# First product of an MLP by seven block products instead of eight, in an encoder block on one core

## The chip, the cores and the metric

The kernel runs on one core of a Trainium2 chip. The metric is the device time of one execution in microseconds (us). Two kernels are compared by the median of several runs of each on the same chip.

The core's engines each work through a queue of their own in order: TensorE (PE, matmul; PEld is its weight load), VectorE (DVE), ScalarE (ACT), GpSimd (POOL), and SyncE (SP), which here only issues transfers. They meet at semaphores. PSUM, where matmuls leave their sums, has eight banks of 128x512 float32.

## The reference

One encoder block on 1536 tokens (512 + 1024) of width 1024, all in float32. Projections, gates and two kinds of attention come first; what the change touches is the end:

```python
merged = sigmoid(ga) * (oa @ w_branch_a) + sigmoid(gb) * (ob @ w_branch_b)
x = x + merged @ w_out
hm = rmsnorm(x, norm_mlp)
u = relu(hm @ w_up)            # 1024 -> 4096
return x + (u * u) @ w_down    # 4096 -> 1024
```

## The kernel before

A float32 product is made of three float16 matmuls: each operand is scaled and split into a high and a low half (`split16`, L924: ACT writes `hi`, DVE writes `lo = scale*src - hi`), and `mm3` (L173) adds hi·hi (L174), hi·lo (L175) and lo·hi (L176) in one PSUM bank. A matmul has 128 rows of weights, up to 512 columns of the moving operand, and a weight load before it.

The program is written as generator functions in one order, and a scheduler with a cost model of its own then sets the order of instructions on each engine's queue. On the chip each queue runs in that order and waits where it must.

The stages after attention, with the trace's times:

- **Branch products** (`branch`, L986; from 1000.30). Six raw weight tiles `st_b0` to `st_b5` are loaded into the pool `raw` (six slots of 128x1024 float32) and split into `w_b` in the pool `w16` (eight slots of [2,1024] float16). `load_o` transposes the attention output and splits it into `u16` and `u16b`.
- **Output projection** (`outproj`, L1009; from 1110.50). It has two halves of 512 output columns, each over three blocks `b` of 512 tokens; `op` matmuls use 512 columns and `y[t] += ...` is one DVE instruction (`add_scaled`, L943). In half 1, from 1173.16, `hnorm(tt)` (L1022) makes the normed rows `hm` of a tile of 128 tokens: two ACT squares with accumulator, small DVE steps, a power on POOL (`hr`), two DVE products. `htrans(tt)` (L1036) turns them: eight 128x128 transposes into two PSUM banks (`hT`), then per bank one ACT copy to `xp` high and one DVE subtraction to `xp` low. The last four tiles' transposes stand inside the first `up`.
- **MLP** (from 1244.33 to the end): a loop over c = 0 to 15, 256 hidden columns each, written as `up(c,0)`, `down_parts(c)`, `up(c,1)`, `up_parts(c+1)`, `up_norms(c+2)`, `down(c)`.
  - `up(c,i)` (L1109): for each block of 512 tokens 8 k-slices times 3 matmuls (72 in all), then for each block ACT `Relu` from PSUM (L1121), ACT square (L1122), ACT copy to `u` high (L1124), DVE subtraction to `u` low (L1125). The temporary `r` comes from the pool `t2` (seven slots of 128x512).
  - `down(c)` (L1127): 12 token tiles times 2 halves; 6 matmuls of 512 columns each into one bank, then `add_scaled` on DVE.
  - `up_norms(c+2)` (L1067): loads two row blocks of w_up as `st_n` (each 512 KB), ACT squares with accumulator (`sq`), one small matmul `nu`, DVE and POOL steps, which give the weights' scale `su` and the row factor `alpha`. `up_parts` (L1086): loads `st_u`, splits into `w_u`, two splits of 128x1024. `down_parts` (L1091): loads `st_d`, squares them, a small matmul `fro_d`, scale `rowd`, splits into `w_d`, two of 128x1024. All these raw tiles share the six `raw` slots, and SP issues their loads in order, each when its slot is free.

Of the kernel before, what the change touches and what calls it, by code (L numbers as in the profile page):

```python
# [130 lines left out]
def encoder(ctx, tc, xt, x, wg, wp, wb, wo, wu, wn, wd, nv, nvr, nmlp, nq, rpb, t5, oneh, negrow, cmask, yp, ys):  # L131
# [781 lines left out]
    with ExitStack() as es:  # L913
# [4 lines left out]
        def tmp(name):  # L918
            return pp.tile([P, 512], F32, tag="t2", bufs=7, name=name)
# [8 lines left out]
        def raw(name, src):  # L928
            st = pp.tile([P, D], F32, tag="raw", bufs=6, name=f"st_{name}")
            xch["last"] = nc.sync.dma_start(out=st, in_=src).ins  # L930
            return st

        def parts(name, st, scale, lo_eng):
            w = pp.tile([P, 2, D], F16, tag="w16", bufs=8, name=f"w_{name}")
            split16(w[:, 0], w[:, 1], st, scale, lo_eng)
            return w

        def squares(acc, st, scale=1.0):
            sq = pp.tile([P, D], F32, tag="sq", bufs=1, name="sq")
# [26 lines left out]
        def load_o(b):  # L966
# [319 lines left out]
```

## Time and profile before

| what | value |
|---|---|
| median of 3 runs | 2255.27 us (2252.01 to 2257.3) |
| the profiled execution: its own time | 2253.47 us |
| its span in the trace | 2251.6 us |
| PE busy | 2132.5 us, 95% |
| DVE, ACT, POOL busy | 1241.7 (55%), 1007.3 (45%), 365.9 us (16%) |
| first `br` matmul, first `op`, `op` half 1, first `up`, last `dn` | 1000.30, 1110.50, 1173.16, 1244.33, 2247.44 us |

How to read it: "busy" is the time in which an engine executes; a matmul's end is modelled, so that two matmuls in a row overlap in the records (each lasts 0.38 us, the next one starts 0.22 us after it). The pace of matmuls is therefore read from their starts. The granted clock is the share of TensorE's full speed (2.4 GHz) that the chip allowed; its lower level is 1.2 GHz. A name such as `up<-xp,w_u` gives output and inputs without buffer numbers. `[3.71 <-ACT sqm L1000]` behind a row says that the engine sat idle 3.71 us before it, and what released it.

### The profile page before, as it was taken

To read this page: it belongs to the slowest core of one execution; us is meant where nothing else is said; L and a number is where in the kernel's file an instruction comes from. 1 tells how busy PE (TensorE), PEld (TensorE's weight loads), DVE (VectorE), ACT (ScalarE), POOL (GpSimd) and SP (SyncE) were. 2 spreads that over 40 slices of the span, in tenths; PEclk is the share of its full clock that TensorE was granted. 3 is DMA by queue.
4 is the path that set the end of the run, shared out by engine and by line. 5 is a ranking of instruction groups with operands and counts; after the bars stand their busy time and mean duration, and the time that the engine had idled before them with its cause. 6 is when DMAs were issued, how large, how long until landed. Compare 5 with 4: busy or idle time off the path is not lost.

```text
span 2251.6 us, 32277 instructions
## 1 busy us (share of the span) xinstructions
PE 2132.5 (95%) x11440; PEld 1087.5 (48%) x11440; DVE 1241.7 (55%) x3135; ACT 1007.3 (45%) x2435; POOL 365.9 (16%) x541
## 2 busy tenths in 40 slices
PE   5899999899989999899999999999999999999999
PEld 3355555465555555344444544444444444444444
DVE  7546767676576577556644644444444444444444
ACT  6346765476566566346532533232333333323222
POOL 5123334244234244100000000000000000000000
PEclk9899999999999999999999999999999999999999
DMA  6676666887776776887530111101111111110002
GB/s 206 208 235 141 138 135 142 172 167 164 160 166 130 164 151 142 184 255 219 164 111 21 56 57 54 36 24 56 57 57 56 56 57 57 56 38 24 34 1 113
DMA packets 342187, 251.23 MB, mean 112 GB/s; under 512 B 210432, under 2 KB 302464, under 8 KB 342024
## 3 DMA queue, kind: packets, MB, share of 16 engines
q1 hardware_dynamic: 341878, 249.15, 42.8%
q8 instruction: 90, 1.47, 0.3%
q14 instruction: 73, 0.60, 0.1%
q10 hardware_dynamic: 146, 0.01, 0.0%
HBM read 164.02 MB, written 53.29 MB: 97 GB/s over the span
## 4 chain that ended last, share of the span: by engine, by line
PE 54%; DMA 1%; issue 1%; ACT 1%; DVE 1%; SPq 0%; POOL 0%; ACTq 0%; DVEq 0%; POOLq 0%
PE up L174 7%; PE dn L174 7%; PE dn L176 7%; PE up L176 7%; PE up L175 7%; PE dn L175 7%; PE op L174 2%; PE op L175 2%; PE op L176 2%; PE br L174 1%; PE br L176 1%; PE br L175 1%; DMA z<-z_d 1%; DMA st_b<-in_wb 0%; PE hT L1041 0%
## 5 line engine op out<-in xcount | busy, mean ns | idle before, releaser
L943 DVE SCALAR_TENSOR_TENSOR y<-dn,und,y 128x512 f32<-128x512 f32 x384 | 287.1, 750 | 179.3 <-PE dn L176 178.9
L1121 ACT ACTIVATE r<-up,alpha 128x512 f32<-128x512 f32 x96 | 65.2, 680 | 591.3 <-PE up L176 591.3
L174 PE MATMUL up<-xp,w_u 128*128 128x512 f16 x768 | 291.0, 379 | 1.0 <-ACT xp L1044 1.0
L176 PE MATMUL dn<-w_d,u 128*128 128x512 f16 x768 | 291.1, 379 | 0.0
L176 PE MATMUL up<-xp,w_u 128*128 128x512 f16 x768 | 291.0, 379 | 0.0
L175 PE MATMUL dn<-w_d,u 128*128 128x512 f16 x768 | 291.0, 379 | 0.0
L175 PE MATMUL up<-xp,w_u 128*128 128x512 f16 x768 | 291.0, 379 | 0.0
L174 PE MATMUL dn<-w_d,u 128*128 128x512 f16 x768 | 291.0, 379 | 0.0
L1125 DVE TENSOR_TENSOR u<-r,u 128x512 f16<-128x512 f32 x96 | 66.4, 692 | 285.1 <-ACT u L1124 281.6
L174 PE MATMUL g<-act,w_g 128*128 128x512 f16 x384 | 147.2, 388 | 21.9 <-ACT act L802 13.0
L175 PE MATMUL g<-act,w_g 128*128 128x512 f16 x384 | 148.3, 386 | 7.6 <-DVE act L803 7.6
L176 PE MATMUL g<-act,w_g 128*128 128x512 f16 x384 | 148.3, 386 | 1.1 <-DVE w_g L263 0.9
L174 PE MATMUL pj1b<-w_p,act 128*128 128x384 f16 x384 | 127.4, 332 | 7.6 <-DVE qn0b L380 4.3
L175 PEld LDWEIGHTS <-act 128*128 128x128 f16 x960 | 96.6, 101 | 70.8 <-issue 19.5
L176 PEld LDWEIGHTS <-act 128*128 128x128 f16 x960 | 96.1, 100 | 66.5 <-issue 7.1
L174 PEld LDWEIGHTS <-act 128*128 128x128 f16 x960 | 97.3, 101 | 63.8 <-issue 6.7
L175 PE MATMUL pj1b<-w_p,act 128*128 128x384 f16 x384 | 127.1, 331 | 0.0
L176 PE MATMUL pj1b<-w_p,act 128*128 128x384 f16 x384 | 127.1, 331 | 0.0
L189 POOL TENSOR_TENSOR f_d<-f_d,mhalf 128x1 f32<-128x1 f32 x16 | 8.9, 556 | 682.8 <-DVE f_d L196 682.8
L174 PEld LDWEIGHTS <-u 128*128 128x128 f16 x768 | 76.3, 99 | 88.9
L174 PEld LDWEIGHTS <-w_u 128*128 128x128 f16 x768 | 76.5, 100 | 88.5
L176 PEld LDWEIGHTS <-u 128*128 128x128 f16 x768 | 75.1, 98 | 90.7
(331 smaller groups left out, 4351.9 us busy)
## 6 DMA issues: line engine op xcount, KB each, us to landing
st_n<-in_wn SPq DMA_DIRECT2D x32, 512.0 KB
st_u<-in_wu SPq DMA_DIRECT2D x32, 512.0 KB
st_d<-in_wd SPq DMA_DIRECT2D x32, 512.0 KB
st_p<-in_wp SPq DMA_DIRECT2D x80, 192.0 KB
z_d<-z SPq DMA_DIRECT2D x48, 256.0 KB
z<-z_d SPq DMA_DIRECT2D x48, 256.0 KB
ba1a<-ba_d SPq DMA_DIRECT2D x12, 768.0 KB
xt<-in_xt SPq DMA_DIRECT2D x24, 256.0 KB
```

The lines of the kernel that those rows point to most:

```text
L174: nc.tensor.matmul(ps, ah, bh, start=first, stop=False)
L175: nc.tensor.matmul(ps, ah, bl, start=False, stop=False)
L176: nc.tensor.matmul(ps, al, bh, start=False, stop=last)
L189: nc.gpsimd.tensor_tensor(out=out, in0=in_, in1=mhalf[:, 0:in_.shape[1]], op=ALU.pow)
L943: nc.vector.scalar_tensor_tensor(out=out, in0=ps, scalar=scale, in1=out, op0=ALU.mult, op1=ALU.add)
L1121: nc.scalar.activation(s, ps[b], AF.Relu, scale=alpha[:, f:f + 1])
L1125: nc.vector.tensor_tensor(out=uu[:, 1, i, tb], in0=s, in1=uu[:, 0, i, tb], op=ALU.subtract)
```

## The change

The first product of the MLP, `up`, is made by Strassen's scheme (Winograd's form): tokens are cut in two halves of 768, the 1024 inputs in two halves of 512, the 256 hidden columns of a c in its two tiles of 128. Seven products of sums of blocks take the place of eight products of blocks. The sums are made in float32 and then split.

- `up(c,j)` now goes over j, two column blocks of 384 tokens of each half. It has seven products of 4 k-slices times 3 matmuls of 384 columns: 84 matmuls, 168 per c (before 144 of 512 columns). Their PSUM results are combined by one ACT copy (L1197) and seven DVE additions of 384 columns (L1193), and `hidden` (L1169 to L1174) does what L1121 to L1125 did, four times per j on 384 columns: three ACT and one DVE instruction each.
- `up_parts(c)` adds four POOL additions or subtractions of 128x512 (`s1` to `s4`) and makes seven splits of 128x512 (an ACT and a DVE instruction each; before two of 128x1024).
- `build(q)` takes the place of `htrans`: six builds of 256 tokens, each with 16 transposes into four banks, one ACT copy (`b12`), four DVE subtractions (`t1` to `t4`), and seven ACT copies to high and seven DVE subtractions to low, all of 128x512. Builds 0 to 3 stand behind the pairs of tiles of output projection half 1, builds 4 and 5 inside `up(0,0)` behind products 6 and 5; `hnorm(10)` and `hnorm(11)` come behind build 4.
- Buffers: `raw` has 4 slots (before 6), `t2` has 6 (7); `w16` 13 of [2,512] (8 of [2,1024]); `sq` is bfloat16. 14 slots `six` hold `u16b`, the output projection's weights and `xp`, and later the seven operands `xs` of each j. Branch weights `b4` and `b5` are loaded when `b0` and `b1` have been split.
- `outproj` takes one PSUM bank per token tile when its turn comes. `down` and its 144 matmuls per c stay, with the token tiles in another order; its weights are split in halves (four splits of 128x512).

```diff
-            return pp.tile([P, 512], F32, tag="t2", bufs=7, name=name)
+            return pp.tile([P, 512], F32, tag="t2", bufs=6, name=name)
...
-            st = pp.tile([P, D], F32, tag="raw", bufs=6, name=f"st_{name}")
+            st = pp.tile([P, D], F32, tag="raw", bufs=4, name=f"st_{name}")
...
+        def build(q):
+
+            tp = {}
+            for h in range(2):
+                for i in range(2):
+                    ps = tp[i, h] = psum(f"hT{2 * q + h}_{i}")
...
+            def out(name, src):
+                p4 = src.rearrange("p (k t) -> p k t", k=4)
+                hi, lo = (xs[name, j][:, l, :, cs] for l in range(2))
                 nc.scalar.activation(hi, p4, AF.Copy)
                 nc.vector.tensor_tensor(out=lo, in0=p4, in1=hi, op=ALU.subtract)
...
+            out("b11", tp[0, 0])
+            b12 = tmp(f"b12_{q}")
+            nc.scalar.activation(b12, tp[0, 1], AF.Copy)
+            t1 = less("t1", b12, tp[0, 0])
+            t2 = less("t2", tp[1, 1], t1)
+            out("t2", t2)
+            out("b21", tp[1, 0])
+            out("t1", t1)
+            t3 = less("t3", tp[1, 1], b12)
+            out("t3", t3)
+            out("b22", tp[1, 1])
+            out("t4", less("t4", tp[1, 0], t2))
...
+            s1 = sum_(tmp(f"s1_{c}"), a21, a22, ALU.add)
+            s2 = sum_(tmp(f"s2_{c}"), s1, a11, ALU.subtract)
+            out(1, a11)
+            out(6, s2)
+            out(2, a12)
+            out(5, s1)
+            s3 = sum_(a21, a11, a21, ALU.subtract)
+            s4 = sum_(a12, a12, s2, ALU.subtract)
+            yield
+            out(7, s3)
+            out(3, s4)
+            out(4, a22)
...
+                ps = psum(f"up{c}_{j}{n}")[:, :384]
+                for k in range(4):
                     kk = slice(k * P, (k + 1) * P)
+                    mm3(ps, w[:, 0, kk], w[:, 1, kk], x7[:, 0, k, :], x7[:, 1, k, :], k == 0, k == 3)
...
+            c11 = t384("c11_")
+            nc.scalar.activation(c11, product7(1), AF.Copy)
+            yield
+            x = add(t384("x_"), product7(6), c11)
+            yield
+            add(c11, product7(2), c11)
+            hidden(c, 0, 0, j, c11)
+            yield
+            p5 = product7(5)
+            yield
+            v = add(t384("v_"), product7(7), x)
+            c22 = add(t384("c22_"), p5, v)
+            add(x, p5, x)
+            hidden(c, 1, 1, j, c22)
+            yield
+            add(x, product7(3), x)
+            hidden(c, 0, 1, j, x)
+            yield
+            add(v, product7(4), v)
+            hidden(c, 1, 0, j, v)
```

Three places in the queues show the order. Names: `hm8_0` is the first half of tile 8's normed rows, `x_t41` the operand t4 of j = 1, `up0_06` product 6 of `up(0,0)`, `hs`, `hr` the norm's small sums and factors; before, `xp0` to `xp2` are the operands of the three token blocks.

PE in the first `up`, before: block 0, then the transposes of tiles 8 and 9 behind the first matmul of block 1.

```order
L176 MATMUL up0_0_14791<-xp0_12805,w_u0_14350 128x512
L174 LDWEIGHTS w_u0_14350 [waits DVE_49]
L174 MATMUL up0_1_14792<-xp1_12806,w_u0_14350 128x512 [waits Activation_49]
L1041 MATMUL hT8_0_14852<-ident_94,hm8_0_14692 128x128 [waits DVE_49,PE_49]
L1041 MATMUL hT8_0_14852<-ident_94,hm8_0_14692 128x128 x3
L1041 MATMUL hT8_1_14859<-ident_94,hm8_1_14693 128x128 [waits DVE_49,PE_49]
L1041 MATMUL hT8_1_14859<-ident_94,hm8_1_14693 128x128 x3
```

PE at the same place after: products 1 and 6 of `up(0,0)`, then the 16 transposes of build 4.

```order
L176 MATMUL up0_06_14928<-x_t20_14353,w_u0_6_14388 128x384
L1057 MATMUL hT8_0_14942<-ident_94,hm8_0_14882 128x128 [waits DVE_49]
L1057 MATMUL hT8_0_14942<-ident_94,hm8_0_14882 128x128 x3
L1057 MATMUL hT8_1_14947<-ident_94,hm8_1_14883 128x128 [waits DVE_49]
L1057 MATMUL hT8_1_14947<-ident_94,hm8_1_14883 128x128 x3
L1057 MATMUL hT9_0_14952<-ident_94,hm9_0_14893 128x128 [waits DVE_49,Activation_49]
```

What stood behind 24 products of block 0 now stands behind the 24 shorter matmuls of products 1 and 6, and waits for `hm8` as before.

DVE ahead of those transposes, before: `hm8` has one low half of `htrans` between the small steps ahead of it and itself.

```order
L1027 TENSOR_TENSOR hs9_14702<-hs9_14702 128x1 [waits Activation_49]
L1028 TENSOR_SCALAR hs9_14702<-hs9_14702 128x1 [waits DVE_49]
L1045 TENSOR_TENSOR xp1_12806<-hT6_0_14763,xp1_12806 128x4x128 [waits PE_49,Activation_49]
L1032 SCALAR_TENSOR_TENSOR hm8_0_14692<-y8_12801,hr8_14698,gm_12653 128x512 [waits Pool_49]
L1032 SCALAR_TENSOR_TENSOR hm8_1_14693<-y8_12801,hr8_14698,gm_12653 128x512
```

DVE at the same place after:

```order
L1069 TENSOR_TENSOR t4_3_14877<-hT6_1_14842,t2_3_14863 128x512
L1065 TENSOR_TENSOR x_t11_14834<-t1_3_14861,x_t11_14834 128x4x128 [waits Activation_49]
L1065 TENSOR_TENSOR x_t31_14836<-t3_3_14871,x_t31_14836 128x4x128 [waits Activation_49]
L1065 TENSOR_TENSOR x_b221_14832<-hT7_1_14852,x_b221_14832 128x4x128 [waits Activation_49]
L1041 TENSOR_TENSOR hs8_14881<-hs8_14881 128x1 [waits Activation_49]
L1065 TENSOR_TENSOR x_t41_14833<-t4_3_14877,x_t41_14833 128x4x128 [waits Activation_49]
L1042 TENSOR_SCALAR hs8_14881<-hs8_14881 128x1 [waits DVE_49]
L1041 TENSOR_TENSOR hs9_14892<-hs9_14892 128x1 [waits Activation_49]
L1042 TENSOR_SCALAR hs9_14892<-hs9_14892 128x1 [waits DVE_49]
L1046 SCALAR_TENSOR_TENSOR hm8_0_14882<-y8_12819,hr8_14888,gm_12653 128x512 [waits Pool_49]
```

The whole of build 3 (eleven DVE instructions, of which the last are shown) now stands ahead of `hm8`.

ACT in the second half of an up, before (c = 5: `up11_0` to `up11_2` are its blocks, `st_n8` the row blocks for c = 8, `st_d14` a down weight of c = 7):

```order
L925 ACTIVATE w_u13_17183<-st_u13_17181,su_12658 128x1024 [waits DMAHW0_49]
L1121 ACTIVATE r11_0_17113<-up11_0_17086,alpha_12657 128x512 [waits PE_49]
L1122 ACTIVATE r11_0_17113<-r11_0_17113 128x512 [waits Activation_49]
L1124 ACTIVATE u16_12652<-r11_0_17113 128x512 [waits Activation_49]
L940 ACTIVATE sq_17613,nu_12655<-st_n8_0_17611 128x1024 [waits DMAHW7_49]
L1121 ACTIVATE r11_1_17142<-up11_1_17087,alpha_12657 128x512 [waits PE_49]
L940 ACTIVATE sq_17617,nu_12655<-st_n8_1_17615 128x1024 [waits DMAHW0_49,Activation_49]
```

ACT at the same place after (c = 5, j = 1; `c11`, `c22` are two of the four results, `st_n7` the row blocks for c = 7, `st_d12` and `st_d13` the down weights of c = 6):

```order
L1197 ACTIVATE c11_5_1_17721<-up5_11_17722 128x384 [waits PE_49]
L925 ACTIVATE w_u6_1_17848<-st_u12_17840,su_12658 128x512 [waits DMAHW7_49]
L944 ACTIVATE sq_17873,nu_12655<-st_n7_0_17871 128x1024 [waits DMAHW1_49]
L1171 ACTIVATE c11_5_1_17721<-c11_5_1_17721,alpha_12657 128x384 [waits DVE_49]
L944 ACTIVATE sq_17877,nu_12655<-st_n7_1_17875 128x1024 [waits DMAHW2_49,Activation_49]
L1172 ACTIVATE c11_5_1_17721<-c11_5_1_17721 128x384 [waits Activation_49]
L1174 ACTIVATE u16_12652<-c11_5_1_17721 128x384 [waits Activation_49]
L944 ACTIVATE sq_18203,nd_12656<-st_d12_18201,nu_12655 128x1024 [waits DMAHW3_49]
L1171 ACTIVATE c22_5_1_17797<-c22_5_1_17797,alpha_12657 128x384 [waits DVE_49]
L944 ACTIVATE sq_18207,nd_12656<-st_d13_18205,nu_12655 128x1024 [waits DMAHW4_49,Activation_49]
```

The squares of `st_n` and `st_d`, with their waits for transfers, now stand between the steps of `hidden`; the norms of a c are taken one c nearer to their use.

## Rows read from the trace of the kernel before

**Rows 1.** First part of the page: busy time, share of the span and instructions of each engine.

```profile
PE 2132.5 (95%) x11440; PEld 1087.5 (48%) x11440; DVE 1241.7 (55%) x3135; ACT 1007.3 (45%) x2435; POOL 365.9 (16%) x541
```

**Rows 2.** Waits of PE from 1000 us to the end: what it waited for, us in total, times, the longest.

```profile
PE fro_m L194 <- ACT sqm L1000: 5.4, 2, 3.7
PE br L175 <- DVE u L926: 1.6, 1, 1.6
PE br L174 <- ACT u L925: 1.2, 1, 1.2
PE up L174 <- ACT xp L1044: 1.0, 1, 1.0
PE hT L1041 <- DVE hm L1032: 1.0, 2, 0.5
```

**Rows 3.** Timeline of PE in a steady `up`: start, modelled duration. The second row here is the 54th start behind the first, with no gap between.

```profile
1514.41 0.38 PE L174 MATMUL up<-xp,w_u 128*128 128x512 f16 x1
...
1526.06 0.38 PE L174 MATMUL up<-xp,w_u 128*128 128x512 f16 x1
```

**Rows 4.** Timeline of PE in the attention stage, matmuls of 384 columns: the second row is the 23rd start behind the first.

```profile
407.43 0.33 PE L174 MATMUL pj0b<-w_p,act 128*128 128x384 f16 x1
...
411.16 0.33 PE L176 MATMUL pj0b<-w_p,act 128*128 128x384 f16 x1
```

**Rows 5.** Costliest groups by line and shape: busy us, mean ns of one, idle before.

```profile
L174 PE MATMUL up<-xp,w_u 128*128 128x512 f16 x768 | 291.0, 379 | 1.0 <-ACT xp L1044 1.0
L174 PE MATMUL pj1b<-w_p,act 128*128 128x384 f16 x384 | 127.4, 332 | 7.6 <-DVE qn0b L380 4.3
```

**Rows 6.** Windows: stretch, length, busy time of PE, PEld, DVE, ACT and POOL with instructions, granted clock, DMA share, GB/s. The first lies in the attention stage, the second in the MLP, the third behind a gap of PE.

```profile
400.00:412.00 12.00, 11.49 (x85) 7.24 (x83) 6.53 (x38) 2.33 (x10) 1.21 (x3) 1.00 0.84 183
1600.00:1660.00 60.00, 60.00 (x283) 27.51 (x281) 26.43 (x44) 19.28 (x30) 1.95 (x3) 1.00 0.17 53
1045.50:1049.00 3.50, 3.50 (x13) 1.50 (x14) 1.67 (x5) 3.09 (x7) 0.55 (x1) 0.70 0.02 6
```

**Rows 7.** Groups by line and shape on DVE, ACT and POOL: busy us, mean ns of one, idle before.

```profile
L943 DVE SCALAR_TENSOR_TENSOR y<-dn,und,y 128x512 f32<-128x512 f32 x384 | 287.1, 750 | 179.3 <-PE dn L176 178.9
L1125 DVE TENSOR_TENSOR u<-r,u 128x512 f16<-128x512 f32 x96 | 66.4, 692 | 285.1 <-ACT u L1124 281.6
L926 DVE SCALAR_TENSOR_TENSOR w_u<-st_u,su,w_u 128x1024 f16<-128x1024 f32 x32 | 39.6, 1280 | 0.0
L1045 DVE TENSOR_TENSOR xp<-hT,xp 128x512 f16<-128x512 f32 x24 | 16.0, 686 | 1.2 <-ACT xp L1044 0.8
L1032 DVE SCALAR_TENSOR_TENSOR hm<-y,hr,gm 128x512 f32<-128x512 f32 x24 | 16.9, 746 | 2.6 <-POOL hr L189 2.6
L380 DVE TENSOR_TENSOR qn1b<-pj1b,rq1b 128x256 f32<-128x256 f32 x48 | 20.1, 419 | 4.1 <-POOL rq1b L375 3.6
L801 DVE TENSOR_TENSOR xt<-xt,rmsr 128x512 f32<-128x512 f32 x18 | 19.9, 1167 | 0.1
L1121 ACT ACTIVATE r<-up,alpha 128x512 f32<-128x512 f32 x96 | 65.2, 680 | 591.3 <-PE up L176 591.3
L244 ACT ACTIVATE wsq<-st_p 128x384 bf16<-128x384 f32 x80 | 41.4, 517 | 39.7 <-DMA st_p<-in_wp 39.1
L925 ACT ACTIVATE w_u<-st_u,su 128x1024 f16<-128x1024 f32 x32 | 34.8, 1133 | 0.0
L814 POOL TENSOR_TENSOR acc<-acc,sqx 128x512 f32<-128x512 f32 x14 | 19.2, 1373 | 5.6 <-ACT sqx L812 5.1
```

**Rows 8.** Timeline of SP in the MLP: when the loads of a round were issued, and the first of the next round.

```profile
1643.73 1.52 SPq L930 DMA_DIRECT2D st_u<-in_wu  x2
1646.12 1.52 SPq L930 DMA_DIRECT2D st_n<-in_wn  x2
...
1706.16 1.52 SPq L930 DMA_DIRECT2D st_u<-in_wu  x2
```

**Rows 9.** Timelines in the MLP: PE's `fro_d` matmul, and the splits of `w_d` that follow it on ACT and DVE (two rounds ahead of rows 8, same place of a round).

```profile
1514.27 0.28 PE L194 MATMUL fro_d<-nd,ones 128*128 128x2 f32 x2
...
1516.38 2.17 ACT L925 ACTIVATE w_d<-st_d,rowd 128x1024 f16<-128x1024 f32 x2
...
1517.55 2.48 DVE L926 SCALAR_TENSOR_TENSOR w_d<-st_d,rowd,w_d 128x1024 f16<-128x1024 f32 x2 [0.35 <-ACT w_d L925]
```

**Rows 10.** Timeline of ACT behind the loads of rows 8: the squares of the first `st_n` and of the second `st_d`.

```profile
1651.33 1.06 ACT L940 ACTIVATE sq<-st_n 128x1024 f32<-128x1024 f32 x1 [3.93 <-DMA st_n<-in_wn]
...
1658.79 1.15 ACT L940 ACTIVATE sq<-st_d,nu 128x1024 f32<-128x1024 f32 x1 [0.85 <-DMA st_d<-in_wd]
```

**Rows 11.** Timelines in output projection half 1: PE's transposes of three tiles, then of the fourth; and one DVE `add_scaled`, with DVE's idle time before it.

```profile
1214.60 2.78 PE L1041 MATMUL hT<-ident,hm 128*128 128x128 f32 x24
1217.88 1.32 PE L1041 MATMUL hT<-ident,hm 128*128 128x128 f32 x8 [0.49 <-DVE hm L1032]
...
1204.44 0.75 DVE L943 SCALAR_TENSOR_TENSOR y<-op,uo,y 128x512 f32<-128x512 f32 x1 [4.43 <-PE op L176]
```

**Rows 12.** Timeline of PE in the branch stage: a gap, and matmuls of 512 columns behind it.

```profile
1045.42 0.39 PE L194 MATMUL fro_m<-msum,ones 128*128 128x8 f32 x2 [3.71 <-ACT sqm L1000]
...
1047.00 0.63 PE L174 MATMUL br<-u16b,w_b 128*128 128x512 f16 x1
...
1049.99 0.54 PE L175 MATMUL br<-u16b,w_b 128*128 128x512 f16 x1
```

More of the change, by code (lines that the diff above doesn't have):

```diff
@@ L1058, in gains @@
         def gains():
[L1060 removed]
+            g2 = pp.tile([P, D], F32, tag="raw", bufs=4, name="g2")
             nc.vector.tensor_tensor(out=g2, in0=gm, in1=gm, op=ALU.mult)
@@ L1082, in up_norms @@
[L1082 to L1089 removed]
+            nc.vector.tensor_reduce(out=t[:, 0:1], in_=ps[:, :2], axis=AX.X, op=ALU.add)
@@ L1146, in encoder @@
         next(lo_)
-        wbs = [raw(f"b{k}", wb[k]) for k in range(6)]
+        wbs = [raw(f"b{k}", wb[k]) for k in range(4)]
         for _ in fill:
@@ L1152, in encoder @@
         sb = scale_b[:, 1:2]
-        wbs = [parts(f"b{k}", w, sb, nc.vector) for k, w in enumerate(wbs)]
+        for k in range(6):
+            wbs[k] = parts(f"b{k}", wbs[k], sb, nc.vector)
+            if k < 2:
+                wbs.append(raw(f"b{k + 4}", wb[k + 4]))
         eg.close()
@@ L1190, in encoder, with slots @@
                 todo, sc = scaled(wo1)
-                so[1] = [parts(*w, nc.vector) for w in todo], sc
+                so[1] = [w for t in todo for w in parts(*t, nc.vector)], sc
         up_norms(0)
-        for b in range(NB):
-            outproj(b, 1)
-            for t in range(4 * b, 4 * b + 4):
-                hnorm(t)
-            if b:
-                for t in range(4 * b - 4, 4 * b):
-                    htrans(t)
-            if b == 0:
-                up_parts(0)
-            if b == 1:
+        first = up_parts(0)
+        def slots(j):
+            for n in X_OF.values():
+                xs[n, j] = six(f"x_{n}{j}", [P, 2, 4, 384])
+        outproj(0, 1)
+        slots(0)
+        for t in range(2):
+            hnorm(t)
+        next(first)
+        for q in range(4):
+            outproj(1 + q // 2, 1, range(q % 2 * 2, q % 2 * 2 + 2))
+            if q == 3:
+                slots(1)
+            build(q)
+            for t in (2 * q + 2, 2 * q + 3):
+                hnorm(t)
+            if q == 1:
                 up_norms(1)
+        for _ in first:
+            pass
         NC = FF // 256
         for c in range(NC):
-            for i in range(2):
-                up(c, i, range(8, 12) if c == i == 0 else ())
-                if i == 0:
+            for j in range(2):
+                for i, _ in enumerate(up(c, j)):
+                    if c == j == 0 and i in (1, 3):
+                        build(4 + i // 2)
+                        if i == 1:
+                            hnorm(10)
+                            hnorm(11)
+                if j == 0:
                     down_parts(c)
             if c + 1 < NC:
-                up_parts(c + 1)
+                for _ in up_parts(c + 1):
+                    pass
             if c + 2 < NC:
```

139 lines of the change are left out of this document (80 added, 59 removed).

## The prediction

> **What bounds the kernel now.** I first read the busy shares: PE 2132.5 us of a span of 2251.6, 95%, DVE 55%, ACT 45%, POOL 16% [rows 1]. A share is an average over stages, so next the waits of PE from the branch products on: 10.2 us of about 1250 in all [rows 2], none of them in the MLP loop behind its first round. There PE sets the end, by the pace at which matmuls start. The timeline gives that pace: 54 starts in 11.65 us, 0.2157 us for 512 columns [rows 3]. A round of the loop (one c) takes 62.43 us [rows 8], and 288 matmuls at 0.2157 are 62.1; a few small ones are the rest. So time leaves this kernel only where PE gets less to do, or loses waits.
>
> **Part 1, the products.** Per c, 144 matmuls of 512 columns go and 168 of 384 come. The reader must not price them by the mean durations: 379 and 332 ns [rows 5] would give 54.6 us before and 55.8 after, a loss of 1.2 us per c. Matmuls overlap in the records, and the pace counts. For 384 columns the attention stage shows it: 23 starts in 3.73 us, 0.1622 [rows 4], at granted clock 1.00 [rows 6], with the same float16 operands and a weight load each. Before: 144 x 0.2157 = 31.06 us; after: 168 x 0.1622 = 27.25; saved 3.81 per c, 16 x 3.81 = 60.9 us. The new matmuls would break even at 31.06/168 = 0.185 us. The `down` half keeps its 144 matmuls (31.06 us); its other token order costs nothing that a row shows. The new round is 62.43 - 3.81 = 58.6 us.
>
> **Part 2, what the other engines must do in a round of 58.6 us.** DVE: 24 `add_scaled` x 0.75, 14 additions of 384 columns at about 0.55 (between 0.42 for 256 columns and 0.69 for 512), 8 low halves of 384 at 0.55, 11 splits of 512 at 0.75 less overlap, small steps: 18 + 8 + 4 + 8 + 2 = 40 us [rows 7]. ACT: 26 passes of 384 at 0.52, 11 splits of 512 at 0.63, 4 squares of 1.06 to 1.15: 25 us [rows 7, 10]. POOL: 4 sums x 1.373 and the powers, 7 us [rows 7]. If POOL's sums slow DVE, the worst row is 1.167 in place of 0.69 for an instruction that ran beside POOL [rows 7]: 4 x 1.4 us of POOL can stretch at most some 8 DVE instructions, +4 us, still under 58.6. No engine becomes the bound on average, so the sums themselves cost nothing while PE's queue covers them. What counts is order.
>
> **Part 3, the steady round by its queues.** I lay it out from T0, where `up(c,1)` begins behind the `fro_d` matmul. Rows 9 show 2.11 us from that matmul to the first split of `w_d`. ACT's four splits of `w_d` then end near T0+4.6, DVE's at about T0+4.7 for the first tile and T0+6.1 for the second (2.48 us for both, begun 1.2 behind ACT [rows 9]). Before, six raw slots let the loads run ahead. With four, `st_n` of c+2 must wait for exactly these slots. In the old trace its first squares began 5.2 us behind the issue, with the pair `st_u` ahead in the queue [rows 8, 10]; without that pair I take 4 us. The pair lands at T0+8.5 and T0+10.2, the second square ends near T0+11.6, and the `nu` matmul stands in PE's queue behind `up(c,1)`, at T0 + 84 x 0.1622 = T0+13.6. Slack: 2 us. The squares of `st_d` of c+1 come behind it on ACT and block the later `hidden` steps until they have landed; I get the last high half at T0+25 to 28, against PE's need of it (the sixth pair of `down` groups, 12 x 1.295 us behind T0+13.8) at T0+29. Slack: 1 to 4 us. I take 0 for both and keep the loss for the range: each microsecond beyond the slack costs 16 us in all. PSUM is the other link: `down` needs banks that only DVE empties, 0.75 of each 1.295 us, so a short block of DVE is caught up by the eight banks.
>
> **Part 4, the start of the MLP.** `build` costs DVE eleven instructions of 0.69 [rows 7], about 0.62 each back to back, 6.8 us for two tiles where `htrans` took 2.7; `hnorm` for two tiles adds 4 x 0.75 and small steps, 3.5. In the projection this fits: two tiles take PE 2 x 24 matmuls = 10.4 us and 1.9 of transposes (2.78 for 24 [rows 11]), against 6.8 + 3.5 + 1.5 (two `add_scaled`) of DVE. But builds 4 and 5 stand inside `up(0,0)`, with only products 1 and 6 (24 matmuls, 3.9 us) ahead of `hT8`. Ahead of `hm8` DVE does all of build 3, `hnorm` of tiles 8 and 9 and an addition: 6.8 + 3.5 + 0.5 = 10.8 us, and a POOL power. PE waits 6 to 7 us. Between builds 4 and 5 the same again: 1.9 + 3.9 us of PE against 6.8 + 3.5 + 0.5 of DVE, 5 us; then `hT11` about 1.6, and the first rounds' norms and additions 3. Sum about 17 us; the old 2.0 us of `hT` and `up` waits there go [rows 2]. The least I can defend is 5 (if ACT and DVE overlap as well as in the old `hT`, 0.5 a wait [rows 11]), the most 25.
> A gap also costs clock. Behind the 3.71 us gap, starts from 1047.00 to 1049.99 come 0.427 us apart, seven steps [rows 12], granted clock 0.70 in that stretch [rows 6]: that is the 1.2 GHz level for a while, 7 x 0.21 = 1.5 us, say 1.7. Two long gaps: 3.4 us (0 to 5).
>
> **Part 5, the branch stage and buffers.** `b4` and `b5` load only after the splits of `b0` and `b1`, and the loads of `z` queue behind them on SP. No row shows that wait; the nearest is a landing of 5.2 us [rows 8, 10], of which the other branch products cover much: 2 us taken, 0 to 5, or -1 at best, since the old 2.8 us of `br` waits [rows 2] come from the same splits. One `t2` slot less, `sq` in bfloat16 and PSUM taken tile by tile in `outproj` change nothing: DVE empties a bank 0.75 us behind PE, which needs 5.18 for the next.
>
> **Sum.** -60.9 + 17 - 2 + 3.4 + 2 = -40.5 us. On the profiled execution's 2253.47 (its span is 2251.6; the 1.9 us around it stay) that is 2213; the median of the runs lies 1.8 us above that execution, so 2215.
>
> **Rivals.**
> 1. *The start is covered.* If DVE is ahead when `up(0,0)` begins, only 5 us of part 4 are left and no clock: 2255.3 - 60.9 + 5 - 2 = 2197. For it: DVE sat idle 4.43 us before each `add_scaled` of the projection [rows 11]; against it: eleven instructions in front of `hm8` in the queue as compiled. Chance 0.10.
> 2. *The round loses part of its gain.* The loads of `st_n` or `st_d` come 0.5 to 2.4 us too late for the slacks of part 3: +8 to +38 us, 2223 to 2253. For it: slacks of 1 to 4 us in sums with terms of 4. Chance 0.20.
> 3. *The four raw slots set the round* (the slower side). The net gain is 40.5/16 = 2.5 us per round; if the second square of `st_n` ends later than T0 + 13.6 + 2.5 = T0+16.1, 4.5 us later than I laid out, the kernel is slower. The old trace has such delays: 3.93 us of ACT idle in front of one square with six slots [rows 10]. A load that takes two more landings costs 5 us, 3 beyond the slack: 2215 + 48 = 2263. Chance 0.09.
> 4. *Shorter matmuls don't pay.* If 384 columns went by the durations' ratio, 332/379 [rows 5], the pace would be 0.189: 168 x 0.189 = 31.7 us, +0.7 per c, +11 us, and with the 20 of parts 4 and 5 it would be 2255.3 + 31 = 2286. Rows 4 speak against it: 0.1622. Chance 0.03.
> The Trainium skill (TensorE: Matmul & The Clock Gate, Back-to-back issue gap) states such a floor, about 81 ns per matmul at 128 columns and 131 at 512 in a sustained stream with weight loads; interpolated, an estimate from that page, 384 columns would take 114, and 2688 of them 307 us against 302 for 2304 of 512, a loss of 5 us. The trace shows 0.2157 and 0.1622 us with weight loads [rows 3, 4], so by this case's rows that rule does not hold; the page's other formula (columns over 2.4 GHz plus 2.5 ns) gives 215.8 and 162.5 ns, as measured.
>
> **Chances.** The forecast, 2207 to 2225, has 0.58 (2206 to 2223), rival 1 0.10, rival 2 0.20, rival 3 0.09, rival 4 0.03. The range goes from rival 1's 2197 to 2246, most of rival 2. About 0.2% (4.5 us) is what a measurement can tell from no change. Faster by more: 0.58 + 0.10 + 0.17 = 0.85; within it 0.03, from the end of rival 2 and the near side of rival 3; slower 0.12.
>
> **What the changed profile would show.** Part 1: starts of `up` 0.1622 apart, the round by SP's issues 58.6 us. Part 3: no wait of PE at `nu` or `dn` behind the first rounds; a wait `nu <- ACT sq` in every round would be rival 2 or 3 by its length, and ACT idle before `sq<-st_n` the sign of the slots. Part 4: two gaps of PE in front of `hT` near the start of `up`, 6 to 7 and 5 us, ended by DVE `hm`, and a stretch at a lower granted clock behind each. Part 5: `br` waits of 3 to 8 us near 1000. The prediction is wrong if the `up` starts are further apart than 0.17, or if a wait returns in every round.

## The result: 41 us faster

The changed kernel takes 2215.34 us (median of 4 runs, 2208.61 to 2218.03) against 2256.22 (4 runs, 2252.01 to 2257.30): ratio 0.9825, 95% interval 0.9803 to 0.9847; the medians differ by 40.9 us. The forecast was 2215. The profiled execution of the changed kernel took 2218.03 us, the longest of its four, with a span of 2216.2; span against span the gain is 35.4 us. Some of the hit is chance: terms of the sum were off in both directions, as the traces show.

### The profile page after: what moved, and what is told of

Read it like the earlier page. It is cut to its first block, busy times and chain, and to the rows that moved or that the text cites. A ratio compares the mean times of both kernels' runs of the same rounds, so it can differ in the third digit from the quotient of the medians.

```text
span 2216.2 us, 33962 instructions
## 1 busy us (share of the span) xinstructions
PE 2080.7 (94%) x11824; PEld 1125.9 (51%) x11824; DVE 1463.2 (66%) x3559; ACT 1098.1 (50%) x2713; POOL 468.7 (21%) x605
## 4 chain that ended last, share of the span: by engine, by line
issue 23%; PE 14%; DVE 8%; DMA 6%; ACT 4%; POOL 2%; SPq 0%; ACTq 0%; DVEq 0%; POOLq 0%
DMA st_n<-in_wn 3%; DVE w_d L926 3%; DMA st_d<-in_wd 2%; ACT sq L944 2%; PE op L174 1%; PE dn L174 1%; PE dn L176 1%; PE op L175 1%; PE op L176 1%; PE dn L175 1%; PE br L174 1%; PE up L174 1%; PE br L175 1%; PE up L175 1%; PE up L176 1%
## 5 line engine op out<-in xcount | busy, mean ns | idle before, releaser
L947 DVE SCALAR_TENSOR_TENSOR y<-dn,und,y 128x512 f32<-128x512 f32 x384 | 271.7, 743 | 60.8 <-PE dn L176 59.4
L1197 ACT ACTIVATE c<-up 128x384 f32<-128x384 f32 x32 | 15.3, 479 | 320.3 <-PE up L176 320.3
L174 PE MATMUL up<-x_t,w_u 128*128 128x384 f16 x512 | 167.9, 328 | 0.0
L175 PE MATMUL up<-x_t,w_u 128*128 128x384 f16 x512 | 167.9, 328 | 0.0
L176 PE MATMUL up<-x_t,w_u 128*128 128x384 f16 x512 | 167.7, 328 | 0.0
L189 POOL TENSOR_TENSOR f_d<-f_d,mhalf 128x1 f32<-128x1 f32 x16 | 12.4, 776 | 554.1 <-DVE f_d L196 554.1
L176 PE MATMUL up<-x_b,w_u 128*128 128x384 f16 x384 | 125.3, 326 | 0.0
L175 PE MATMUL up<-x_b,w_u 128*128 128x384 f16 x384 | 125.3, 326 | 0.0
L174 PE MATMUL up<-x_b,w_u 128*128 128x384 f16 x384 | 125.3, 326 | 0.0
L175 PEld LDWEIGHTS <-u 128*128 128x128 f16 x768 | 75.1, 98 | 91.5 <-issue 3.7
```

Source lines behind the costliest of these rows:

```text
L174: nc.tensor.matmul(ps, ah, bh, start=first, stop=False)
L175: nc.tensor.matmul(ps, ah, bl, start=False, stop=False)
L176: nc.tensor.matmul(ps, al, bh, start=False, stop=last)
L189: nc.gpsimd.tensor_tensor(out=out, in0=in_, in1=mhalf[:, 0:in_.shape[1]], op=ALU.pow)
L947: nc.vector.scalar_tensor_tensor(out=out, in0=ps, scalar=scale, in1=out, op0=ALU.mult, op1=ALU.add)
L1197: nc.scalar.activation(c11, product7(1), AF.Copy)
```

## The profile after

The first part of the page, changed kernel (compare [rows 1]):

```profile
PE 2080.7 (94%) x11824; PEld 1125.9 (51%) x11824; DVE 1463.2 (66%) x3559; ACT 1098.1 (50%) x2713; POOL 468.7 (21%) x605
```

PE is still the busiest engine; DVE is busy 222 us longer than before. The waits of PE from 995 us to the end (compare [rows 2]):

```profile
PE hT L1057 <- DVE hm L1046: 10.8, 4, 4.8
PE fro_m L194 <- ACT sqm L1011: 7.5, 2, 5.8
PE br L175 <- DVE u L926: 2.6, 1, 2.6
PE br L174 <- ACT u L925: 1.4, 1, 1.4
PE nu L1112 <- ACT sq L944: 1.3, 4, 0.4
PE dn L174 <- DVE y L947: 0.7, 3, 0.3
```

Two of these places were foreseen (`hT` and `br`); `fro_m` has grown, and `nu` and `dn` are new. The view lists the longer waits only; the short gaps at `nu` and in `dn` are read from the starts in the timeline, of which one round is shown below.

Where the time went is seen by stage. One view lists, per tile name, the first and last start on PE; `dn` of the kernel before, then the four of the changed kernel:

```profile
L174 PE MATMUL dn<-w_d,u x768: 376/379/379, 1280.3 to 2247.0; 128*128 128x512 f16 x192
```

```profile
L174 PE MATMUL br<-u,w_b x96: 376/380/634, 998.1 to 1112.9; 128*128 128x512 f16 x96
L174 PE MATMUL op<-wo,xp x96: 376/379/380, 1113.6 to 1175.5; 128*128 128x512 f16 x96
L174 PE MATMUL up<-x_t,w_u x512: 325/326/528, 1248.3 to 2180.6; 128*128 128x384 f16 x171
L174 PE MATMUL dn<-w_d,u x768: 376/379/380, 1294.2 to 2211.6; 128*128 128x512 f16 x192
```

From such rows, in us (the third stretch holds the `up` of 15 rounds and the `down` of all 16; stretches are called by the letters below; one profiled execution each):

| kernel | A: first `br` to first `op` | B: first `op` to first `dn` | C: first to last `dn` |
|---|---|---|---|
| before | 110.2 | 169.8 | 966.7 |
| changed | 115.5 | 180.6 | 917.4 |
| e1 eight products | 114.0 | 181.0 | 970.0 |
| e2 sums on DVE | 114.5 | 180.1 | 909.9 |
| e3 norms first | 113.2 | 181.3 | 910.0 |
| e4 fewer low halves | 112.3 | 177.6 | 917.9 |
| e5 late builds | 112.8 | 180.0 | 920.6 |
| e6 seven `t2` | 114.5 | 177.6 | 922.9 |
| e7 late weight splits | 105.4 | 179.9 | 916.7 |
| e8 = e2 + e7 | 106.3 | 179.2 | 910.0 |
| e9 = e3 + e7 | 106.2 | 181.4 | 910.0 |
| e10 eight `t2` | 108.9 | 179.3 | 926.1 |
| e11 low halves on ACT | 112.4 | 181.2 | 917.2 |
| e12 eight `t2`, norms ahead of builds | 109.5 | 174.5 | 925.2 |

Changed against before: A +5.3, B +10.8, C -49.3, and the start of A 2.2 earlier; sum -35.4. The start of A scatters from 993.1 to 1002.3 over the profiles of the changed kernels, whose matmuls up to there are the same: a single run's time says little below 5 us, a stretch says more.

The pace of `up`, 26 starts apart (compare [rows 3, 4]):

```profile
1635.94 0.33 PE L174 MATMUL up<-x_b,w_u 128*128 128x384 f16 x1
...
1640.17 0.33 PE L176 MATMUL up<-x_b,w_u 128*128 128x384 f16 x1
```

4.23/26 = 0.1627 us, with times of two decimals 0.1623 to 0.1631. One round, by what happens behind its `fro_d` matmul at 1635.32 (T0 = 1635.46; compare [rows 8 to 10]), on DVE, POOL, SP, ACT and PE in this order (the first fence line is four splits merged, the second is the second of them alone):

```profile
1639.25 4.76 DVE L926 SCALAR_TENSOR_TENSOR w_d<-st_d,rowd,w_d 128x512 f16<-128x512 f32 x4
...
1639.92 1.76 DVE L926 SCALAR_TENSOR_TENSOR w_d<-st_d,rowd,w_d 128x512 f16<-128x512 f32 x1
...
1639.38 1.76 POOL L1135 TENSOR_TENSOR s<-s,st_u 128x512 f32<-128x512 f32 x1 [0.94 <-POOL s L1135]
1641.10 1.71 POOL L1135 TENSOR_TENSOR st_u<-st_u,st_u 128x512 f32<-128x512 f32 x1
...
1641.71 2.66 SPq L930 DMA_DIRECT2D st_n<-in_wn  x2
...
1645.26 1.06 ACT L944 ACTIVATE sq<-st_n 128x1024 bf16<-128x1024 f32 x1 [3.22 <-DMA st_n<-in_wn]
...
1648.14 1.06 ACT L944 ACTIVATE sq<-st_n 128x1024 bf16<-128x1024 f32 x1 [1.22 <-DMA st_n<-in_wn]
...
1648.94 0.33 PE L176 MATMUL up<-x_t,w_u 128*128 128x384 f16 x1
1649.34 0.38 PE L1112 MATMUL nu<-nu,ones 128*128 128x2 f32 x2
```

`nu` starts 0.40 behind the last `up` where 0.16 would do: a gap of 0.24 us. The second square of `st_n` began at T0+12.7, not T0+10.5, because DVE's four splits of `w_d` ended at T0+8.6, not T0+6.1. They took 1.19 us each on average: the two that began while one of POOL's sums ran took 1.75 us, the other two 0.75.

The start of the loop, PE (compare [rows 11]) and its stretches as windows (busy time of PE, PEld, DVE, ACT, POOL, then the granted clock), with the matmuls behind the last gap:

```profile
1255.18 3.69 PE L1057 MATMUL hT<-ident,hm 128*128 128x128 f32 x16 [4.77 <-DVE hm L1046]
...
1267.14 1.94 PE L1057 MATMUL hT<-ident,hm 128*128 128x128 f32 x8 [4.36 <-DVE hm L1046]
1270.39 1.94 PE L1057 MATMUL hT<-ident,hm 128*128 128x128 f32 x8 [1.31 <-DVE hm L1046]
...
1272.44 0.53 PE L175 MATMUL up<-x_t,w_u 128*128 128x384 f16 x1
1272.76 0.53 PE L176 MATMUL up<-x_t,w_u 128*128 128x384 f16 x1
```

```profile
1244.00:1272.00 28.00, 17.19 (x97) 12.54 (x96) 24.97 (x47) 17.28 (x39) 2.80 (x5) 0.82 0.12 38
1272.00:1276.00 4.00, 4.00 (x16) 1.96 (x15) 3.75 (x7) 3.00 (x6) 0.00 (x0) 0.54 0.00 0
1255.00:1259.00 4.00, 3.81 (x18) 3.43 (x19) 3.96 (x8) 1.79 (x3) 0.54 (x1) 0.57 0.00 0
1267.00:1272.00 5.00, 3.55 (x16) 3.21 (x17) 3.87 (x8) 1.68 (x3) 0.55 (x1) 0.50 0.01 3
```

Two gaps of 4.8 and 4.4 us where 6 to 7 and 5 were foreseen, ended by `hm`, and a third of 1.3; DVE is busy 25 of the 28 us. Behind the third gap eleven starts of `up` lie 0.32 us apart, at the 1.2 GHz level (granted clock 0.54 of 2.4 GHz): 11 x 0.16 = 1.8 us. The 32 transposes behind the three gaps ran at that level too (0.57 and 0.50): by their starts they took 3.5 + 1.7 + 1.7 us, where 32 at the 24 in 2.78 us of [rows 11] take 3.7. That is 3.3 us more, an estimate from these rows; with the 1.8 the lower clock cost about 5 us here.

The long wait in the branch stage: SP's loads, ACT, and PE.

```profile
1077.87 0.33 SPq L1001 DMA_DIRECT2D z<-z_d  x1
1079.13 2.31 SPq L930 DMA_DIRECT2D st_o<-in_wo  x2
1081.77 2.31 SPq L1001 DMA_DIRECT2D z<-z_d  x3
...
1073.04 5.00 ACT L925 ACTIVATE wo<-st_o,f_o 128x512 f16<-128x512 f32 x8
...
1083.19 0.63 ACT L1002 ACTIVATE z<-z 128x512 f32<-128x512 f32 x1 [2.98 <-DMA z<-z_d]
1083.73 0.61 ACT L1011 ACTIVATE sqm<-y 128x512 bf16<-128x512 f32 x1
...
1084.48 0.59 PE L194 MATMUL fro_m<-msum,ones 128*128 128x8 f32 x2 [5.77 <-ACT sqm L1011]
```

All eight splits of the first projection weights stand together on ACT; the loads of the second weights (`st_o`) wait in SP's queue for their raw slots, the loads of `z` stand behind them, and the last squares that `fro_m` needs come late. In the kernel before, this place had the splits of two of the four weight tiles; the other two came behind the loop. Of the 5.3 us by which stretch A grew, 3.1 are the waits inside it (`fro_m` 7.5 us for 5.4, `br` on DVE 2.6 for 1.6); the other 2.2 go with the granted clock of the whole stretch, 0.93 where it was 0.97. The stretch as a window, before, changed and in e7 (below):

```profile
1000.30:1110.50 110.20, 103.15 (x486) 48.92 (x486) 78.97 (x122) 73.87 (x142) 1.65 (x3) 0.97 0.69 224
```

```profile
998.10:1113.60 115.50, 105.36 (x487) 49.59 (x487) 84.61 (x134) 75.29 (x148) 2.19 (x4) 0.93 0.66 216
```

```profile
993.10:1098.50 105.40, 100.97 (x486) 48.46 (x486) 83.58 (x134) 73.41 (x146) 2.59 (x4) 0.98 0.73 236
```

## The experiments

Each kernel is the changed one with the edit shown. Ratios are to the kernel before on the same chip, with 95% intervals; the changed kernel itself has 0.9825 (0.9803 to 0.9847). Of e1 to e9 only e1 and e8 have an interval that lies wholly outside that one; for the others the whole time alone does not tell them from the changed kernel, and what the edit does is read from the stretches and waits. e10 to e12 are single executions for their traces, without a ratio.

**e1: an eighth product.**

```diff
-                for k in range(4):
+                m = 8 if n == 1 else 4
+                for kt in range(m):
+                    k = kt % 4
```

> Product 1 is made twice in its bank, so that each half of an up has eight products; the result holds product 1 doubled, all other instructions stay. Theory (the gain is the time that PE's matmuls take at their pace): 24 more matmuls of 384 columns per round at 0.1622 us, 16 x 3.89 = +62 us, less some 4 to 7 us because the waits of PE in each round are covered by the longer half: 2270 us (2264 to 2279), slightly slower than the kernel before; round 62.5 to 63.0 us. Rival (the gain came from something else, such as the smaller splits or the order of loads): the time rises by less than 30 us, under 2245.

Measured: 2270.41 us, ratio 1.0087 (1.0072 to 1.0102). C is 970.0 us, 52.6 more than in the changed kernel: 15 x 24 x 0.1627 = 58.6, less some 6 us of gaps, since those at `nu` are gone. The gain comes and goes with the eighth product's matmuls; the rival falls.

**e2: the sums on DVE.**

```diff
-                nc.gpsimd.tensor_tensor(out=o, in0=a, in1=b, op=op)
+                nc.vector.tensor_tensor(out=o, in0=a, in1=b, op=op)
```

> The four sums of weight blocks of a round go from POOL to DVE. In the changed kernel's trace the four splits of w_d took DVE 4.76 us while POOL made its sums beside them, where 0.74 each was seen elsewhere. Theory (POOL's sums slow DVE's splits, and so the loads of st_n): the splits take 2.7 to 3.0 us, the wait of PE at nu (0.13 to 0.6 us a round) goes, the round falls from 59.1 to 58.6 to 58.9: 2207 to 2212. Rival (the four raw slots alone set the wait): splits shorter, but the wait at nu stays at 0.2 to 0.5 us; with four more instructions on DVE 2214 to 2225.

Measured: 2207.43 us, 0.9809 (0.9794 to 0.9823). No wait at `nu` or `dn` is left; C is 909.9, 7.5 less than in the changed kernel. The rival falls by the waits; the gain in the whole time, 0.0016 of the ratio, lies inside the intervals. Groups by line and shape in the changed kernel, in e2, and in e3 (below): the splits of `w_d` on DVE, mean ns of one over all rounds.

```profile
L926 DVE SCALAR_TENSOR_TENSOR w_d<-st_d,rowd,w_d 128x512 f16<-128x512 f32 x64 | 72.7, 1194 | 0.2
```

```profile
L926 DVE SCALAR_TENSOR_TENSOR w_d<-st_d,rowd,w_d 128x512 f16<-128x512 f32 x64 | 43.9, 748 | 0.8
```

```profile
L926 DVE SCALAR_TENSOR_TENSOR w_d<-st_d,rowd,w_d 128x512 f16<-128x512 f32 x64 | 73.1, 1201 | 0.2
```

**e3: norms written first.**

```diff
+            if c + 2 < NC:
+                up_norms(c + 2)
             if c + 1 < NC:
                 for _ in up_parts(c + 1):
                     pass
-            if c + 2 < NC:
-                up_norms(c + 2)
```

> In the loop the norms for c+2 are written ahead of the weights for c+1, so that st_n takes its raw slots ahead of st_u. Theory (the order in which the four raw slots are handed out sets the wait at nu and the blocked ACT queue): the wait of PE at nu goes, ACT's waits for transfers between the steps of hidden shrink, PE's waits in down go too: round 58.6, 2207 (2204 to 2211). Rival (another load then stands in the same place): a wait of 0.2 us or more a round remains, at nu, up or dn: 2213 or more.

Measured: 2214.85 us, 0.9836 (0.9821 to 0.9852): the whole time shows no gain and misses the forecast. The stretches do show it: C is 910.0, no gap at `nu` or `dn`, although the splits still take 1201 ns on average beside POOL. In this profile A started 4.2 us later than in the changed kernel, and the waits at `hT` were 12.4 us for 10.8. The longer waits at `hT` return in e9, which has the same edit (12.3 us), so they are probably its price; why is not shown. So the wait at `nu` needs both: slots handed out so that `st_n` waits for the splits of `w_d`, and splits that POOL slows. Either cure is worth some 7.5 us of C; neither is clear of the intervals in the whole time.

**e4: fewer low halves.** The condition leaves the low halves of t1 to t4 out in builds 3 to 5.

```diff
-                nc.vector.tensor_tensor(out=lo, in0=p4, in1=hi, op=ALU.subtract)
+                if q < 3 or name in ("b11", "b21", "b22"):
+                    nc.vector.tensor_tensor(out=lo, in0=p4, in1=hi, op=ALU.subtract)
+                elif cs.start == 0:
+                    nc.gpsimd.memset(xs[name, j][:, 1], 0.0)
```

> Left out: the low halves of the four computed operands (t1 to t4) in builds 3 to 5, 12 DVE instructions of about 0.62 us; four fills on POOL take their place once, so the products use zeros there. Theory (the start of the MLP is bound by DVE's throughput): PE's waits at hT, 10.8 us in the changed kernel, fall by 6 to 8 us, and the stretch at the lower clock behind them gets shorter: 2206 to 2210. Rival (the waits are latency, from the squares over POOL's power to hm): they fall by under 2 us, 2213 to 2216.

Measured: 2211.56 us, 0.983 (0.9814 to 0.9847); waits at `hT` 8.1 us, B 3.0 shorter. Between the two theories: 2.7 us less waiting for some 7.4 us less work of DVE.

**e5: builds 4 and 5 later.**

```diff
-                    if c == j == 0 and i in (1, 3):
-                        build(4 + i // 2)
-                        if i == 1:
+                    if c == j == 0 and i in (3, 5):
+                        build(4 if i == 3 else 5)
+                        if i == 3:
```

> Builds 4 and 5 stand behind products 5 and 3 of up(0,0), in place of 6 and 5. Theory (DVE's throughput is short between the end of the projection and the end of the builds, and PE's 84 matmuls of up(0,0), 13.6 us, are the only cover): two more products (3.9 us) stand ahead of the first transposes and the same number between the two builds, so the first gap of PE (4.8 us) falls to about 1 us, the second and third stay, since DVE's work is the same: the sum of the waits at hT, 10.8 us, falls by 3 to 4 us, the clock loss with it by 0 to 1.8; the branch stage and the rounds stay: 2209 to 2213. Rival (what is not waited for at hT is waited for later, at the first products of up(0,1) or at nu): less than 1 us.

Measured: 2220.30 us, 0.9856 (0.9831 to 0.9881). The waits at `hT` fell to 7.7 us as the theory said, but PE then waited at `nu` behind `up(0,1)`, and the granted clock fell behind that gap:

```profile
1292.57 0.58 PE L1112 MATMUL nu<-nu,ones 128*128 128x2 f32 x2 [3.57 <-ACT sq L944]
```

```profile
1290.00:1300.00 10.00, 7.43 (x22) 3.02 (x23) 5.32 (x13) 9.16 (x19) 2.93 (x3) 0.66 0.35 112
```

B is 180.0, only 0.6 less, and C, in which most of that slow stretch lies, is 3.2 longer. The rival was right for the time.

**e6: seven slots of t2, twelve of w16.**

```diff
-            return pp.tile([P, 512], F32, tag="t2", bufs=6, name=name)
+            return pp.tile([P, 512], F32, tag="t2", bufs=7, name=name)
...
-                w = pp.tile([P, 2, 512], F16, tag="w16", bufs=13, name=f"w_{name}_{i}")
+                w = pp.tile([P, 2, 512], F16, tag="w16", bufs=12, name=f"w_{name}_{i}")
```

> The pool t2 gets its seventh slot back, and w16 goes from 13 to 12 slots to pay for it. Theory (the long wait at fro_m, 5.8 us where 1.7 was, comes from the eight splits of the projection's weights in one place and the loads of z that stand behind the loads of st_o): the wait stays at 4 to 6 us, and the branch stage at 115 us. Rival (the loads of z wait for a slot of t2): the wait falls to about 2 us, and the stage to 111.

Measured: 2220.96 us, 0.9867 (0.9837 to 0.9897). The wait at `fro_m` stayed (6.3 us): not the slots of `t2`. B gained 3.0 us, C lost 5.5, with longer gaps at `nu` (7.4 us in the view of waits for 1.3). Here both pools changed; e10 below, with eight slots of `t2` and `w16` as it was, loses 8.7 us of C. Why more slots of `t2` lengthen the rounds is not shown.

**e7: the projection weights split later.**

```diff
-                if b == 1 and c == 5:
+                if b == 2 and c == 1:
                     todo, sc = scaled(wo0)
```

> The eight splits of the first projection weights stand behind the norm factor of block 1 (branch of block 2, behind column 1), in place of column 5 of block 1. Theory (these splits delay the squares that the factor needs): the second wait at fro_m falls from 5.8 to under 2.5 us, and the branch stage from 115 to about 111: 2211. Rival (slots of t2, or the late loads of b4 and b5): it stays at 4 to 6 us.

Measured: 2210.47 us, 0.9806 (0.9776 to 0.9837); the profiled execution, 2201.48, was the fastest of its four. PE's waits in e7:

```profile
PE hT L1057 <- DVE hm L1046: 10.2, 4, 4.8
PE br L175 <- DVE u L926: 2.6, 1, 2.6
PE br L174 <- ACT u L925: 2.1, 1, 2.1
PE fro_m L194 <- ACT sqm L1011: 1.8, 2, 1.6
```

`fro_m` fell from 7.5 us to 1.8 in all, and A to 105.4: 10.1 below the changed kernel, more than forecast, and 4.8 below the kernel before. Of the 10.1, 5.7 are the wait; the rest goes with the granted clock, 0.98 for 0.93. The edit moves the splits, and with them the freeing of the slots for `st_o`; which of the two delays, ACT's work or the loads of `z` behind `st_o`, weighs more is not separated. The waits at `br`, 4.7 us where the kernel before had 2.8 [rows 2], are all that is left for the late loads of `b4` and `b5`: at most 2 us, and no run tried these alone.

**e8 and e9: the cures together** (e2 with e7, e3 with e7; their diffs are shown).

> The sums on DVE and the late splits of the projection weights together. Theory (the loss in the rounds, 7.5 us, and that at fro_m, some 6 to 9 us, are independent, since they lie in different stages): both go, 2215.3 x (1 - 0.0016 - 0.0035) is about 2203, ratio to the kernel before 0.975 to 0.980. Rival (one gives back the other's, through the order that the scheduler then makes): no better than the better of the two, 0.980 to 0.983.

> The norms written first, sums still on POOL, and the late splits of the projection weights. Theory: the same 0.975 to 0.980 as with the sums on DVE, since the loads then have slack of their own and DVE's slower splits beside POOL cost PE nothing. Rival (POOL's sums cost PE time in the rounds some other way): a ratio above e8's by more than 0.002.

Measured: e8 2200.58 us, 0.9771 (0.9750 to 0.9792); e9 2204.16, 0.9782 (0.9760 to 0.9803). Both forecasts held; with slack for the loads, POOL's sums make no difference that these intervals show. e8 has the lowest time here, 0.55% below the changed one by the ratios (0.9771/0.9825); e9 does not differ from it beyond the intervals.

**e10: eight slots of t2.** The gain tile is left out to make room.

```diff
-            return pp.tile([P, 512], F32, tag="t2", bufs=6, name=name)
+            return pp.tile([P, 512], F32, tag="t2", bufs=8, name=name)
...
-                                               in1=gm[:, i * 512:(i + 1) * 512], op0=ALU.mult, op1=ALU.mult)
+                                               in1=y[tt][:, i * 512:(i + 1) * 512], op0=ALU.mult, op1=ALU.mult)
```

> Left out: the gain norm_mlp (hm is multiplied by y in its place, by the same instruction, and the gain's maximum is a constant), which frees room for two more slots of t2, eight in all. At issue: why the start of the MLP waits. Theory (a chain: hm needs slots of t2, which the t1 to t4 of the build before hold until their low halves are made, so hm comes only behind the whole build): the sum of the waits at hT falls from 10.8 us to 3 to 6. Rival (DVE's throughput alone): it stays at 8 us or more.

Measured, in a single execution: 2223.06 us, 9.7 us at `hT`, B 179.3. The chain through slots of `t2` falls, since two more slots hardly shorten the waits; DVE was busy 26.2 of the 28 us from 1244.

**e11: low halves on ACT.**

```diff
-                nc.vector.tensor_tensor(out=lo, in0=p4, in1=hi, op=ALU.subtract)
+                if q < 3 or name in ("b11", "b21", "b22"):
+                    nc.vector.tensor_tensor(out=lo, in0=p4, in1=hi, op=ALU.subtract)
+                else:
+                    nc.scalar.activation(lo, p4, AF.Copy)
```

> In builds 3 to 5 ACT makes the low halves of the computed operands t1 to t4, as copies of their sources in place of the differences (their values are wrong, so the products of j = 1 are): DVE has 12 instructions of about 0.62 us less there, ACT 12 more. Read in the stretch from the first matmul of the projection to the first of down, 180.6 us in the changed kernel, with 10.8 us of waits at hT. Theory (DVE's throughput bounds the start): the stretch is 174 to 177 us, the waits 4 to 7 us. Rival (a chain of latency from transposes over ACT and POOL to hm): 179 us or more, the waits 9 us or more; ACT as the next bound would lie between.

Measured, in a single execution: 2216.55 us, 11.4 us at `hT` behind `hm`, B 181.2, both in the rival's range. In the 28 us from 1244 DVE's work fell to 19.4 us and ACT's rose to 20.9; the waits did not fall. DVE's throughput alone is refuted as the cause. In the trace ACT, with DVE relieved, had nearly the whole build in front of the squares of the next `hm`; whether that order or a chain of latency holds `hm` back, the next run asks.

**e12: norms ahead of builds**, on e10.

```diff
-            build(q)
             for t in (2 * q + 2, 2 * q + 3):
                 hnorm(t)
+            build(q)
...
-                        build(4 + i // 2)
                         if i == 1:
                             hnorm(10)
                             hnorm(11)
+                        build(4 + i // 2)
```

> As the run with eight slots of t2 (the gain left out, hm multiplied by y), and in addition the norms of the next two tiles are written ahead of each build, also ahead of build 4, so that hm8 to hm11 stand ahead of most of builds 3 and 4 in the queues of DVE and ACT. Beside the run with eight slots, whose stretch from the first matmul of the projection to the first of down took 179.3 us with 9.7 us of waits at hT. Theory (PE waits because a whole build stands ahead of the next norm, whichever engine is the slower at it): the waits at hT fall to under 4 us and the stretch to 171 to 176 us, with some new waits at the first products of up(0,1). Rival (the sum of the work of DVE sets it whatever the order): the waits turn up elsewhere in up(0,0) or up(0,1) and the stretch stays at 178 us or more.

Measured, in a single execution: 2215.02 us. PE's waits at `nu` and at `hT` from 990 us to the end, e12:

```profile
PE nu L1104 <- ACT sq L942: 12.3, 12, 6.2
...
PE hT L1055 <- DVE hm L1044: 2.3, 1, 2.3
```

The waits at `hT` fell from 9.7 to 2.3 us, B from 179.3 to 174.5, both as the theory said: with the same norms and nearly the same work (DVE busy 27.8 of the 28 us from 1244), what stands ahead of the norm in the queues decides. 6.2 us came back at the `nu` behind `up(0,1)`, whose squares were late. A kernel with this order, the gain kept, and e8's cures was not made.

## Why the prediction was right, and where it was not

- **The products (part 1): right.** 60.9 us forecast from the pace of 0.1622. The pace read above is 0.1627, or 16 x 3.73 = 59.6; e2 and e3, whose rounds have no gaps, gain 56.8 us over 15 rounds, 3.79 each, or 60.6. e1 gives the eighth product back and the gain is gone. Rival 4, and the rule of the Trainium skill beside it (TensorE: Matmul & The Clock Gate, Back-to-back issue gap), are refuted by the pace in this kernel too.
- **The engines in a round (part 2): right on average.** In 1600 to 1660 the window shows DVE busy 41.2 us, ACT 25.2, POOL 9.1 of 60, against 40, 25 and 7 per round of 58.6.
- **The steady round (part 3): the slack was mis-sized.** "Slack: 2 us" became about -0.2 in the round shown. With e2's 56.8 us as the full gain, C lost 56.8 - 49.3 = 7.5 us, in gaps of up to 0.6 at `nu` in every round and some in `dn`. The failing term is the end of DVE's splits, T0+6.1, measured T0+8.6. Part 2 saw that POOL's sums might slow DVE (1.167 for 0.69 [rows 7]; an instruction beside a sum took 1.75) and asked only whether DVE's average would still fit; the price was not put into the chain of part 3. e2 and e3 show the two halves of the cause. This is a small rival 2, 0.5 us a round. By the prediction's own sign, "a wait returns in every round", this part was wrong; the time stayed in its range because the waits are short. The gaps in `dn`, where the eight banks were to catch up, go with both cures; how they arise is not shown.
- **The start (part 4): right in place, 4 us too dear, and wrong on its parts.** 17 + 3.4 - 2 = 18.4 forecast; B grew by 10.8 although it holds one `up`, 3.8 us shorter: 14.6. The waits were taken too long: 17 us for `hT` and the first norms, measured 10.8 at `hT` and, as what is left of the 14.6, about 0.7 elsewhere (10.8 + 5.1 + 0.7, less the 2.0 of old waits). The clock was taken too cheap, 5.1 us against 3.4, because the slow transposes were not counted. The place of the reason holds: what stands ahead of `hm` in the queue makes PE wait (e12, one execution). But it is not DVE's queue alone: e11 took work off DVE, and the waits stayed, with ACT's queue in its place.
- **The branch stage (part 5): wrong in mechanism.** 2 us forecast for late `b4` and `b5`, 5.3 measured. The step that failed is what was left out: the eight weight splits, which the change put together in one place, with the loads of `z` behind `st_o`, and the clock behind the longer waits. e7 takes 10.1 us off A; e6 shows that a slot more of `t2` does not.
- **The sum.** +0.3 (pace), +7.5 (rounds), -3.8 (start), +3.3 (branch), -2.2 (ahead of A): the traces differ by 35.4, 5 less than the 40.5 forecast. The medians differ by 40.9, since the profiled execution after was 2.7 us above its median and the one before 2.8 below. The time was right by a sum whose large term was right, and whose small errors and scatter cancelled; that it came out at 2215 to the microsecond is luck.

## What to carry to other kernels

Price matmuls by the distance of their starts, not by their modelled durations: here the two give opposite signs. When work is given to an idle engine, ask whom it slows and put that into the chain with the least slack, not into an average. Behind a gap of PE, count everything that runs at the lower clock, transposes too. And look at the whole diff for work that it only moves: taking eight splits out of one place gave back 10.1 us, more than the 7.5 that the new sums cost the rounds.

## What the runs showed of the hardware

A split on DVE whose two inputs lie in SBUF took about 0.75 us with none of POOL's sums beside it (748 ns on average in e2), and 1.75 when it began while a sum ran, as at 1639.92. The sums that began while a split ran took 1.76 and 1.71 us. An `add_scaled`, whose one input is PSUM, took 0.75 us although a sum began 0.23 us behind its start, and that sum took 1.27 (changed kernel, DVE and POOL):

```profile
2127.61 0.75 DVE L947 SCALAR_TENSOR_TENSOR y<-dn,und,y 128x512 f32<-128x512 f32 x1
...
2127.84 1.27 POOL L1135 TENSOR_TENSOR st_u<-st_u,s 128x512 f32<-128x512 f32 x1 [11.54 <-DVE w_u L926]
```

The Trainium skill (GPSIMD Engine Reference, Specifications) says that GpSimd shares its SBUF interfaces with VectorE and contends with instructions that have two SBUF inputs; this trace agrees, and shows the price on both sides.
